# Causal attention on one core: one key tile for up to four query tiles a step, value products up to 512 columns wide

## The chip, the cores and the metric

The kernel runs on one core of a Trainium2 chip. The time is device microseconds of one execution; before the change three runs took 2228.47, 2224.61 and 2228.84, median 2228.47. The core's engines run side by side, each through its own queue in order: TensorE (PE; its weight loads are shown apart as PEld), VectorE (DVE), ScalarE (ACT), GpSimd (POOL), and SyncE (SP), whose queue issues nearly all DMAs. They wait for each other by semaphores.

## The reference, cut to what matters

Two layers over 1024 tokens of width 1024; layer 0 mixes by gating and convolution, layer 1 by attention with 16 heads of width 64, and each is followed by a convolutional feed-forward part. The change touches the attention alone:

```python
def dilated_attention(q, k, v):
    outs, lses = [], []
    for window, dilation in DILATED_PATTERNS:      # (128, 1), (512, 4), (2048, 16)
        o, lse = dilated_branch(q, k, v, window, dilation)
        outs.append(o)
        lses.append(lse)
    wts = jax.nn.softmax(jnp.stack(lses, axis=0), axis=0)
    return jnp.einsum('pbsh,pbshd->bshd', wts, jnp.stack(outs, axis=0))

# in the odd layer
qkv = (h @ odd_w_qkv[j]).reshape(bn, s, 3, ATTN_HEADS, HEAD_DIM)
q = rotary(qkv[:, :, 0], pos)
k = rotary(qkv[:, :, 1], pos)
v = qkv[:, :, 2]
o = dilated_attention(q, k, v).astype(x.dtype).reshape(bn, s, D_MODEL)
x = x + o @ odd_w_o[j]
```

Each branch is a softmax over the earlier keys at its distances, and the branches are mixed by their sums. That is one causal softmax in which a key counts as often as branches reach it; the kernel adds the logarithm of that count to the scores (the tile `mask`).

## The kernel before, in words

Nothing is scheduled by a compiler: the order on each engine is the order in which the Python code emits instructions. A `Ticker` counts ticks, and `after(n, fn)` emits `fn` n ticks later. A "unit" is a slice of independent matrix work (6 or 9 products of 512 columns) that is put between the parts of the attention as filler; `feed(x)` emits as many units as add up to x.

Float32 values are split for TensorE into a rounded high part (ACT, `hi_of`, line 196) and the rest (DVE, `lo_of`); products of two such values take three matmuls, and the value product below takes two, since v's parts stand side by side in the 128 weight columns.

The heads are taken in 8 pairs `hp`, and in each pair the heads e = 0 and 1. For each of these 16 passes:

- `scores` (lines 1431 and 1432) multiplies a query tile of 128 rows with all its earlier keys into PSUM banks `pss`; DVE adds the mask and takes the maximum (`top`), ACT takes the exponential (`ex`), and the tile `p` holds 128 queries by up to 1024 keys.
- `turn` transposes blocks of 128 x 128 of `p` through TensorE into a bank `ppt` (lines 1498, 1499). ACT and DVE split that bank into `tt`: the rounding one tick later, the rest two ticks later, which is ahead of the next step's transposes.
- `value` multiplies v with `tt` into a bank `po` (line 1518), two steps (`VLAG`) after the `turn`.

Before the change a step (hp, e, j, g) takes two query tiles (2j and 2j + 1) and two key tiles, so a value product has 256 columns and a step has four; 10 steps make a pass, in the order j = 3, 2, 0, 1. Where a block lies wholly above the diagonal it is zeroed by a POOL memset. The scores of a pair j are emitted four and three steps ahead of its first step. A step has two ticks, and each is fed with 0.6 units, 24 units a pair of heads.

The filler of a pair is the preparation of the next pair (`prepare`): 8 units each for k, q and v. After k's last unit `rotate` issues four DMAs on SP that bring the swapped halves into `sw`; six ticks later DVE multiplies `sw` with the sine, then the tile itself with the cosine (`rk` or `rq`), adds both, and ACT and DVE split the sum into `rh` and `rl`. For k, eight DMAs then make stacked copies; for q, four. k's rotation falls into the second head of a pair, q's into the first head of the next pair. During the seventh pair three `o` tiles are loaded back (`ot`), split on ACT and POOL (`o_split`), and in the last pair the filler is the first part of the output product (`psd`).

`stile` takes SBUF tiles from one pool of 23 (`p`, `tt`, the q and v of two pairs, raw weights, `sw` and more), and `bank` PSUM banks from a pool of 8. A new tile's first writer waits for the last reader of the tile that had the place before.

Of the kernel before, what the change touches and what calls it, by code (L numbers as in the profile page):

```python
# [58 lines left out]
LAST_RATE = 0.6  # L59
# [76 lines left out]
def block_kernel(ctx, tc, io, out):  # L136
# [1164 lines left out]
    def attention(x_dram, hT, then, late):  # L1301
# [113 lines left out]
        def scores(hp, e, qi, p):  # L1415
# [30 lines left out]
            def ex():  # L1446
# [6 lines left out]
        JORDER = (3, 2, 0, 1)  # L1453
        steps = [(hp, e, j, g) for hp in range(KT) for e in range(2) for j in JORDER
                 for g in range(j + 1)]
        first = {}
        for gi, (hp, e, j, g) in enumerate(steps):
            first.setdefault((hp, e, j), gi)
        LEAD = 4
        VLAG = 2  # L1460
# [6 lines left out]
        def do_scores(hp, e, j, odd):  # L1467
            n0, n1 = P * (2 * j + 1), P * (2 * j + 2)
            if not odd:
                if n0 + n1 <= S:  # L1470
                    t = stile(name="p")
                    ptiles[(hp, e, j)] = (t[:, :n0], t[:, n0:n0 + n1])
                else:
                    ptiles[(hp, e, j)] = (stile(name="p")[:, :n0], None)
            elif ptiles[(hp, e, j)][1] is None:
                ptiles[(hp, e, j)] = (ptiles[(hp, e, j)][0], stile(name="p")[:, :n1])
            scores(hp, e, 2 * j + odd, ptiles[(hp, e, j)][odd])
# [5 lines left out]
        def turn(hp, e, j, g):  # L1483

            pa, pb = ptiles[(hp, e, j)]
            last = 2 * j + 1
            pt = bank("ppt")
            tt = stile([P, 2, HALF], F32R, name="tt")
            tts[(hp, e, j, g)] = tt
            c = 0  # L1490
            for n, kb in enumerate(key_order(j, g)):
                ks = slice(kb * P, (kb + 1) * P)
                if kb == last:

                    c = P
                    pool.memset(f32v(tt[:, :, 0:P]), 0.0)
                else:
                    nc.tensor.transpose(pt[:, 256 * n:256 * n + P], pa[:, ks], ident)  # L1498
                nc.tensor.transpose(pt[:, 256 * n + P:256 * n + 256], pb[:, ks], ident)  # L1499
# [3 lines left out]
        def key_order(j, g):  # L1503
            return (2 * g + 1, 2 * g) if g == j else (2 * g, 2 * g + 1)

        def value(hp, e, j, g):
            v2 = sets[hp]["v"][e]
            half = j // 2
# [362 lines left out]
```

## Time and profile before

| what | before |
|---|---|
| runs, us | 2228.47, 2224.61, 2228.84 |
| the profiled execution | 2228.55 |
| its span | 2226.8 |
| granted clock of TensorE, mean | 0.995 |
| attention, first score product to last value product | 1036.8 to 1518.6 us of the span |
| value products (line 1518) | 640 of 256 columns |
| transposes for them (lines 1498, 1499) | 576 |
| splits of turned tiles, on ACT and on DVE | 160 and 160 |
| zeroing of blocks on POOL | 64, 312 ns each |

The profile is one execution. Its page gives busy times of the engines and the costliest groups; in a timeline each row has its start, its length, the engine, line and operation, the tiles written and read, and in brackets the idle time of the engine just before it with what ended it. A row for DVE names line 128, since a helper emits them all; they are told apart by tiles.

### The profile page before, as it was taken

What the parts mean: (1) busy time and instruction counts of PE and PEld (TensorE: products, weight loads), DVE (VectorE), ACT (ScalarE), POOL (GpSimd) and SP (SyncE); (2) the same over time, 40 slices, a digit from 0 to 9 for tenths busy, and PEclk for the clock granted to TensorE, in tenths of its full rate; (3) what the DMA queues carried; (4) which work ended last, traced back from release to release, by engine and by line L of the source; (5) the groups of instructions that cost most, each with busy time, mean ns of one, the idle gap of its engine ahead of it and who ended that gap; (6) DMA issues with size and microseconds to landing.
All of it is one profiled execution on the core that took longest, in us unless ns stands there. A gap on an engine that the chain in (4) does not pass through costs nothing.

```text
span 2226.8 us, 29232 instructions
## 1 busy us (share of the span) xinstructions
PE 2179.1 (98%) x10448; PEld 1822.1 (82%) x10448; DVE 1611.4 (72%) x2578; ACT 1096.7 (49%) x1667; POOL 700.8 (31%) x538
## 2 busy tenths in 40 slices
PE   7999899999999999999999999999999999999998
PEld 6888678888888888878888888788888888888886
DVE  6998668877777764665777777786787777778555
ACT  5345265544444445353555555554654444444532
POOL 0122023766665430040000000102466666653001
PEclk9999999999999999999999999999999999999999
DMA  5478411353534598446344444632134444349933
GB/s 191 113 134 184 161 67 67 133 183 128 181 142 158 175 352 321 142 168 152 94 106 116 124 106 122 187 126 97 67 133 156 171 144 178 132 158 347 363 131 116
DMA packets 138833, 352.13 MB, mean 158 GB/s; under 512 B 16448, under 2 KB 16832, under 8 KB 138688
## 3 DMA queue, kind: packets, MB, share of 16 engines
q1 hardware_dynamic: 133072, 329.90, 44.2%
q0 software_dynamic: 5616, 20.36, 4.6%
q8 instruction: 82, 1.34, 0.2%
q14 instruction: 63, 0.52, 0.1%
HBM read 216.01 MB, written 100.64 MB: 142 GB/s over the span
## 4 chain that ended last, share of the span: by engine, by line
PE 49%; DVE 2%; issue 2%; ACT 1%; POOL 0%; DMA 0%; SPq 0%; DVEq 0%; POOLq 0%; ACTq 0%
PE psd L1245 9%; PE psu L259 4%; PE psu L260 4%; PE psu L258 4%; PE po L1518 3%; PE psb L1069 3%; PE psb L1066 3%; PE psb L1067 3%; PE psc L1067 2%; PE psc L1069 2%; PE psc L1066 2%; PE pss L1432 2%; PE pss L1431 2%; PE ppt L1499 1%; PE ppt L1498 1%
## 5 line engine op out<-in xcount | busy, mean ns | idle before, releaser
L1245 PE MATMUL psd<-ab 128*128 128x512 f32 x1800 | 410.1, 389 | 0.0
L1245 PEld LDWEIGHTS psd<-ab 128*128 128x128 f32 x1800 | 337.5, 188 | 69.9
L258 PE MATMUL psu<-hTh,w 128*128 128x512 f32 (+1 forms) x592 | 236.9, 400 | 2.0 <-ACT hTh L196 2.0
L260 PE MATMUL psu<-hTh,w 128*128 128x512 f32 (+1 forms) x592 | 229.5, 388 | 0.0
L259 PE MATMUL psu<-hTl,w 128*128 128x512 f32 (+1 forms) x592 | 229.1, 387 | 0.2 <-DVE hTl L128 0.2
L196 ACT CAST ab<-ab 128x1024 fp32r<-128x1024 f32 x150 | 156.0, 1051 | 139.4 <-PE psd L1245 59.2
L128 DVE TENSOR_TENSOR ab<-ab,ab 128x1024 fp32r<-128x1024 f32 x150 | 192.1, 1334 | 33.4 <-ACT ab L196 33.0
L128 DVE TENSOR_TENSOR x<-psd,x 128x512 f32<-128x512 f32 x152 | 102.1, 686 | 136.7 <-PE psd L1245 110.1
L128 POOL MEMSET tt<- 128x256 f32 x64 | 19.9, 312 | 457.9 <-PE po L1518 260.8
L1103 ACT COPY sn<-psb 128x512 f32<-128x512 f32 x120 | 70.2, 586 | 170.2 <-PE psb L1069 127.4
L128 POOL TENSOR_TENSOR y<-y,y 128x512 f32<-128x512 f32 x66 | 95.6, 1448 | 182.5 <-DMA act<-y 116.4
L196 ACT CAST tt<-ppt 128x512 fp32r<-128x512 f32 (+1 forms) x160 | 86.6, 541 | 97.2 <-PE ppt L1499 87.6
L128 DVE TENSOR_TENSOR tt<-ppt,tt 128x512 fp32r<-128x512 f32 (+1 forms) x160 | 101.2, 633 | 45.8 <-ACT tt L196 44.6
L260 PEld LDWEIGHTS psu<-hTh,w 128*128 128x128 f32 x592 | 112.0, 189 | 23.1
L258 PEld LDWEIGHTS psu<-hTh,w 128*128 128x128 f32 x592 | 112.4, 190 | 19.0 <-ACT hTh L196 2.2
L259 PEld LDWEIGHTS psu<-hTl,w 128*128 128x128 f32 x592 | 112.6, 190 | 17.5 <-DVE hTl L128 0.5
L128 POOL TENSOR_TENSOR sm<-sm,mhalf 128x1 f32<-128x1 f32 (+2 forms) x38 | 31.2, 821 | 282.3 <-DVE sm L128 282.3
L128 POOL TENSOR_TENSOR s<-wr 128x512 f32<-128x512 f32 x40 | 83.0, 2076 | 116.8 <-DVE psa L128 100.8
L128 DVE TENSOR_TENSOR wl<-wr,wh 128x1024 fp32r<-128x1024 f32 x88 | 119.2, 1355 | 0.0
L1448 ACT ACTIVATE p<-p,sma 128x896 f32<-128x896 f32 (+7 forms) x128 | 99.5, 778 | 35.4 <-DVE sma L128 34.6
L128 DVE TENSOR_TENSOR pse<-psc,sn 128x512 f32<-128x512 f32 x40 | 27.9, 699 | 117.1 <-ACT sn L1103 117.1
L1518 PE MATMUL po<-tt,v 128*128 128x256 f32 x640 | 108.8, 292 | 3.8 <-DVE tt L128 2.9
(252 smaller groups left out, 5854.4 us busy)
## 6 DMA issues: line engine op xcount, KB each, us to landing
wr<-in_w_up_dram SPq DMA_DIRECT2D x88, 512.0 KB, 4.4
ab<-act SPq DMA_DIRECT2D x154, 256.0 KB, 5.4
act<-y SPq DMA_DIRECT2D x66, 512.0 KB, 2.9
wq<-in_w_down_dram SPq DMA_DIRECT2D x44, 512.0 KB, 5.3
wt<-wq SPq DMA_DIRECT2D x44, 512.0 KB, 4.6
ab<-wt SPq DMA_DIRECT2D x88, 256.0 KB, 5.4
ab<-in_w_down_dram SPq DMA_DIRECT2D x66, 256.0 KB, 5.6
wr<-in_w_qkv_dram SPq DMA_DIRECT2D x24, 512.0 KB, 3.8
```

Source lines behind the costliest of these rows:

```text
L128: return fn(*args, **kw)
L196: nc.scalar.copy(hi, src)
L258: nc.tensor.matmul(out_ap, st[0], mv[0], start=first, stop=False)
L259: nc.tensor.matmul(out_ap, st[0], mv[1], start=False, stop=False)
L260: nc.tensor.matmul(out_ap, st[1], mv[0], start=False, stop=last)
L1066: nc.tensor.matmul(ps, st[0], mv[0], start=f, stop=False, skip_group_check=True)
L1067: nc.tensor.matmul(ps, st[0], mv[1], start=False, stop=False, skip_group_check=True)
L1069: nc.tensor.matmul(ps, st[1], mv[0], start=False, stop=e, skip_group_check=True)
L1103: nc.scalar.copy(self.sn[key], self.b)
L1245: nc.tensor.matmul(ps, a[:, c], b[:, HALF:D], start=first and k == 0, stop=last and k == 2, skip_group_check=True)
L1448: nc.scalar.activation(p, p, AF.Exp, bias=sm[:, 2:3], scale=0.125, accum_out=lsum[hp][:, c:c + 1])
L1518: nc.tensor.matmul(po[:, c], v2[:, kb, :], tt[:, z, 256 * n:256 * n + 256], start=(g == 0 and n == 0 and z == 0), stop=(g == j and n == 1 ...
```

## The change

A step (hp, e, half, kb) now takes one key tile `kb` for all query tiles of a half (four tiles of 128, 512 queries) that can see it. The upper half has 8 steps and comes first, the lower half 4, so a pass has 12. A value product is 512 columns wide, and narrower towards the diagonal: 512 six times a pass, 384 twice, 256 four times, two products each. One block a half is zeroed, where 128 columns are left (the product then is 256 wide). `S_LEADS` says how many steps before a half's first step the scores of its four query tiles are emitted: 6, 5, 4, 3 for the upper half (tile 7 first), 5, 4, 3, 3 for the lower. The filler is fed by `shares`: a step with more work of its own (estimated in `work`) gets less; the sum over a pair stays 24 units, now over 24 steps or 48 ticks. In the last pair the shares are scaled by `LAST_RATE`. The steps of `finish_pair` are moved by two ticks.

```diff
-LAST_RATE = 0.6
+LAST_RATE = 0.5
+
+
+S_LEADS = ((5, 4, 3, 3), (6, 5, 4, 3))
+VLAG = 2
...
-        JORDER = (3, 2, 0, 1)
-        steps = [(hp, e, j, g) for hp in range(KT) for e in range(2) for j in JORDER
-                 for g in range(j + 1)]
+        steps = [(hp, e, half, kb) for hp in range(KT) for e in range(2)
+                 for half in (1, 0) for kb in range(4 * half + 4)]
...
-        for (hp, e, j), gi in first.items():
-            s_at.setdefault(gi - LEAD, []).append((hp, e, j, 0))
-            s_at.setdefault(gi - LEAD + 1, []).append((hp, e, j, 1))
+        for (hp, e, half), gi in first.items():
+            for n, lead in enumerate(S_LEADS[half]):
+                s_at.setdefault(gi - lead, []).append((hp, e, 4 * half + 3 - n))
...
-            c = 0
-            for n, kb in enumerate(key_order(j, g)):
-                ks = slice(kb * P, (kb + 1) * P)
-                if kb == last:
-
-                    c = P
-                    pool.memset(f32v(tt[:, :, 0:P]), 0.0)
-                else:
-                    nc.tensor.transpose(pt[:, 256 * n:256 * n + P], pa[:, ks], ident)
-                nc.tensor.transpose(pt[:, 256 * n + P:256 * n + 256], pb[:, ks], ident)
+            q0 = max(4 * half, kb)
+            c = (q0 - 4 * half) * P
+            if kb == 4 * half + 3:
+
+
+                pool.memset(f32v(tt[:, :, 2 * P:3 * P]), 0.0)
+            for qi in range(q0, 4 * half + 4):
+                at = (qi - 4 * half) * P
+                nc.tensor.transpose(pt[:, at:at + P],
+                                    ptiles[(hp, e, qi)][:, kb * P:(kb + 1) * P], ident)
             after(1, lambda: hi_of(tt[:, 0, c:], pt[:, c:]))
             after(2, lambda: lo_of(tt[:, 1, c:], pt[:, c:], tt[:, 0, c:]))
...
-            for n, kb in enumerate(key_order(j, g)):
-                for z in range(2):
-                    nc.tensor.matmul(po[:, c], v2[:, kb, :], tt[:, z, 256 * n:256 * n + 256],
-                                     start=(g == 0 and n == 0 and z == 0),
-                                     stop=(g == j and n == 1 and z == 1))
+            c = min(2, max(4 * half, kb) - 4 * half) * P
+            tt = tts.pop((hp, e, half, kb))
+            for z in range(2):
+                nc.tensor.matmul(po[:, c:], v2[:, kb, :], tt[:, z, c:],
+                                 start=kb == 0 and z == 0, stop=kb == last and z == 1,
+                                 skip_group_check=True)
...
             after(1, a)
-            after(2, b)
-            after(3, c)
-            after(4, d)
-            after(9, f)
+            after(4, b)
+            after(5, c)
+            after(6, d)
+            after(11, f)
...
-        per_tick = n_units / 40.0
+        n_steps = len(steps) // KT
+
+        def work(gi):
+            hp, e, half, kb = steps[gi % len(steps)]
+            n = 4 * half + 4 - max(4 * half, kb)
+            w = n * 0.09 + 2 * max(n, 2) * 0.057
+            return w + sum(0.114 * (a[2] + 1) for a in s_at.get(gi, ()))
+        base = KT // 2 * n_steps
+        works = [work(base + i) for i in range(n_steps)]
+        total = (sum(works) + n_units * 1.36) / n_steps
+        shares = [max(0.0, total - w) for w in works]
+        shares = [x * n_units / sum(shares) / 2 for x in shares]
```

On TensorE, around the end of the upper half in pass 8 (a transpose writes `ppt`, a value product `po`, a score product `pss`, filler `psu`), before the change:

```order
L258 MATMUL psu_10325<-hTh_7734,w_10009 128x512
L259 MATMUL psu_10325<-hTl_7735,w_10009 128x512
L260 MATMUL psu_10325<-hTh_7734,w_10009 128x512
L1518 MATMUL po_10186<-tt_10260,v_1430_9754 128x256 x4
L1431 MATMUL pss_10343<-k_9484,st_9728 128x512
L1432 MATMUL pss_10343<-k_9484,st_9728 128x512
L1431 MATMUL pss_10346<-k_9484,st_9728 128x512
L1432 MATMUL pss_10346<-k_9484,st_9728 128x512
L1499 MATMUL ppt_10355<-ident,p_10194 128x128
L1498 MATMUL ppt_10355<-ident,p_10194 128x128
L1499 MATMUL ppt_10355<-ident,p_10194 128x128
```

and now, where step 7's single transpose and step 8's four follow each other:

```order
L1497 MATMUL ppt_10294<-ident,p_9928 128x128
L1511 MATMUL po_10150<-tt_10232,v_1456_9724 128x384 x2
L1435 MATMUL pss_10306<-k_9425,st_9625 128x512
L1436 MATMUL pss_10306<-k_9425,st_9625 128x512
L1435 MATMUL pss_10309<-k_9425,st_9625 128x256
L1436 MATMUL pss_10309<-k_9425,st_9625 128x256
L1497 MATMUL ppt_10316<-ident,p_10204 128x128 x2
L1497 MATMUL ppt_10316<-ident,p_10155 128x128 x2
```

A step had four value products of 256 columns and filler about it; now the steps at the end of a half are short, and two sets of transposes stand close together.

On DVE, where the rotation of q stands in pass 8 (`sw` with the sine, `rq` with the cosine, `tt` the splits of turned tiles, the rows with `p` and `pss` the maxima), before the change:

```order
L128 TENSOR_TENSOR sw_10209<-sw_10209,sin_7723 128x1024
L128 TENSOR_TENSOR rq_10074<-rq_10074,cos_7722 128x1024
L128 TENSOR_TENSOR tt_10286<-ppt_10285,tt_10286 128x512
L128 ISA p_10306,sma_10307<-pss_10308,mask_7721 128x512
L128 ISA sma_10307 128x1
L128 ISA p_10306,sma_10307<-pss_10311,mask_7721,sma_10307 128x384
L128 ISA sma_10307 128x1
L128 TENSOR_SCALAR sma_10307<-sma_10307 128x1
L128 TENSOR_TENSOR o_9742<-o_9742,r_10251 128x1024
L128 TENSOR_TENSOR rq_10074<-rq_10074,sw_10209 128x1024
```

and now:

```order
L132 TENSOR_TENSOR sw_10109<-sw_10109,sin_7723 128x1024
L132 TENSOR_TENSOR rq_10037<-rq_10037,cos_7722 128x1024
L132 TENSOR_TENSOR tt_10164<-ppt_10163,tt_10164 128x512
L132 ISA p_10155,sma_10180<-pss_10181,mask_7721 128x384
L132 ISA sma_10180 128x1
L132 TENSOR_SCALAR sma_10180<-sma_10180 128x1
L132 TENSOR_TENSOR rq_10037<-rq_10037,sw_10109 128x1024
L132 TENSOR_TENSOR tt_10191<-ppt_10190,tt_10191 128x512
```

The same rotation now stands in the first half of the pass, behind the split of step 2 and ahead of those of steps 3 and 4; before it stood behind the maxima of the next half's scores, in the sixth of ten steps. The four DMAs that fill `sw` stand on SP behind the eight copies of k in both.

At the end of pass 15, TensorE before the change:

```order
L1518 MATMUL po_13097<-tt_13182,v_1963_12402 128x256 x4
L1498 MATMUL ppt_13225<-ident,p_13140 128x128
L1499 MATMUL ppt_13225<-ident,p_13140 128x128
L1498 MATMUL ppt_13225<-ident,p_13140 128x128
L1499 MATMUL ppt_13225<-ident,p_13140 128x128
L1518 MATMUL po_13097<-tt_13202,v_1963_12402 128x256 x4
L1499 MATMUL ppt_13242<-ident,p_13140 128x128
L1498 MATMUL ppt_13242<-ident,p_13140 128x128
L1499 MATMUL ppt_13242<-ident,p_13140 128x128
L1518 MATMUL po_13248<-tt_13214,v_1963_12402 128x256 x4
L1518 MATMUL po_13248<-tt_13226,v_1963_12402 128x256 x4
L1518 MATMUL po_13248<-tt_13243,v_1963_12402 128x256 x4
```

and now:

```order
L1497 MATMUL ppt_13053<-ident,p_12770 128x128
L1511 MATMUL po_12963<-tt_13032,v_2021_12292 128x384 x2
L1497 MATMUL ppt_13061<-ident,p_13013 128x128 x2
L1497 MATMUL ppt_13061<-ident,p_12968 128x128 x2
L1511 MATMUL po_12963<-tt_13043,v_2021_12292 128x256 x2
L1497 MATMUL ppt_13071<-ident,p_13013 128x128
L1497 MATMUL ppt_13071<-ident,p_12968 128x128 x2
L1511 MATMUL po_12963<-tt_13054,v_2021_12292 128x256 x2
L1497 MATMUL ppt_13082<-ident,p_12968 128x128 x2
L1511 MATMUL po_13086<-tt_13062,v_2021_12292 128x512 x2
L1497 MATMUL ppt_13091<-ident,p_12968 128x128
L1511 MATMUL po_13086<-tt_13072,v_2021_12292 128x384 x2
```

In both no filler stands among the last steps; four such steps before, seven now, with fewer columns each. On POOL the zeroing of step 7's tile (`tt_13054`) stands behind the last split of an `o` tile.

More of the change, by code (lines that the diff above doesn't have):

```diff
@@ L1451, in scores, with do_scores @@
             after(2, ex, 2)
-        JORDER = (3, 2, 0, 1)
-        steps = [(hp, e, j, g) for hp in range(KT) for e in range(2) for j in JORDER
-                 for g in range(j + 1)]
+        steps = [(hp, e, half, kb) for hp in range(KT) for e in range(2)
+                 for half in (1, 0) for kb in range(4 * half + 4)]
         first = {}
[L1457 to L1460, printed above, removed]
+        for gi, (hp, e, half, kb) in enumerate(steps):
+            first.setdefault((hp, e, half), gi)
         s_at = {}
-        for (hp, e, j), gi in first.items():
-            s_at.setdefault(gi - LEAD, []).append((hp, e, j, 0))
-            s_at.setdefault(gi - LEAD + 1, []).append((hp, e, j, 1))
+        for (hp, e, half), gi in first.items():
+            for n, lead in enumerate(S_LEADS[half]):
+                s_at.setdefault(gi - lead, []).append((hp, e, 4 * half + 3 - n))
         ptiles = {}
[L1467 to L1472, printed above, removed]
-                else:
[L1474 to L1477, printed above, removed]
+        def do_scores(hp, e, qi):
+            n = P * (qi + 1)
+            if qi >= 4:
+                ptiles[(hp, e, qi)] = stile(name="p")[:, :n]
+            elif qi % 2:
+                t = stile(name="p")
+                ptiles[(hp, e, qi)] = t[:, :n]
+                ptiles[(hp, e, qi - 1)] = t[:, n:2 * n - P]
+            scores(hp, e, qi, ptiles[(hp, e, qi)])
         tts = {}
@@ L1500, in turn, with value @@
             after(1, lambda: hi_of(tt[:, 0, c:], pt[:, c:]))
             after(2, lambda: lo_of(tt[:, 1, c:], pt[:, c:], tt[:, 0, c:]))
-        def key_order(j, g):
-            return (2 * g + 1, 2 * g) if g == j else (2 * g, 2 * g + 1)
-        def value(hp, e, j, g):
+        def value(hp, e, half, kb):
             v2 = sets[hp]["v"][e]
-            half = j // 2
-            new = j in (3, 0) and g == 0
-            if new:
+            last = 4 * half + 3
+            if kb == 0:
                 pos[0] = bank("po")
@@ L1522, in value @@
+            tt = tts.pop((hp, e, half, kb))
[3 more added lines that the diff above has]
+                                 skip_group_check=True)
+            if kb == last:
                 if hp not in outs_o:
@@ L1527, in ev @@
                     vec.tensor_tensor(o, po[HD:P, :], o, op=ALU.add)
-                    if e == 1 and j == 1:
+                    if e == 1 and half == 0:
                         finish_pair(hp)
@@ L1624, in attention @@
         tk.until(lambda: "v" in sets[0])
-        for gi in range(-LEAD, 0):
+        for gi in range(-max(S_LEADS[1]), 0):
             for a in s_at.get(gi, ()):
@@ L1647, in attention @@
         for step in steps[-VLAG:]:
-            feed(2 * per_tick)
+            feed(2 * LAST_RATE)
             tick(2)
```

20 lines of the change are left out of this document (7 added, 13 removed).

## The prediction

> **What bounds the kernel now.** I read the page first, then the busy time of the engines by stretches of the attention stage.
>
> ```profile
> span 2226.8 us, 29232 instructions
> PE 2179.1 (98%) x10448; PEld 1822.1 (82%) x10448; DVE 1611.4 (72%) x2578; ACT 1096.7 (49%) x1667; POOL 700.8 (31%) x538
> ...
> PEclk9999999999999999999999999999999999999999
> ```
>
> The execution took 2228.55 us by the clock of the runs, 1.75 more than its span and 0.08 over the median of 2228.47. All my sums start from 2228.55. TensorE is busy 98% at full clock, so the order of the other engines counts only where it leaves TensorE waiting.
>
> ```profile
> 1340.00:1400.00 60.00, 60.00 (x353) 52.19 (x352) 45.48 (x104) 34.89 (x72) 2.18 (x7) 1.00 0.44 110
> 1400.00:1460.00 60.00, 54.47 (x307) 47.12 (x306) 46.94 (x98) 34.69 (x67) 10.26 (x10) 0.94 0.76 227
> 1460.00:1520.00 60.00, 58.95 (x363) 51.57 (x362) 44.24 (x113) 35.67 (x73) 12.45 (x14) 1.00 0.20 63
> ```
>
> After the stretch and its length come PE, PEld, DVE, ACT and POOL, then clock and DMA. In the normal stretch PE never idles, DVE has 14.5 us of 60 free and ACT 25. Idle time exists in pass 12 (the seventh pair's first head; I number the 16 passes from 0) and at the end of pass 15. So a normal pass can gain only through fewer streamed columns, and any new wait is a loss.
>
> **Term 1, the matmuls.** A busy row overlaps the next one, so I take start to start.
>
> ```profile
> 1423.96 0.65 PE L1518 MATMUL po<-tt,v 128*128 128x256 f32 x4
> 1424.44 0.40 PE L1431 MATMUL pss<-k,st 128*128 128x512 f32 x1
> 1424.68 0.40 PE L1432 MATMUL pss<-k,st 128*128 128x512 f32 x1
> 1424.91 0.34 PE L1431 MATMUL pss<-k,st 128*128 128x384 f32 x1
> 1425.09 0.34 PE L1432 MATMUL pss<-k,st 128*128 128x384 f32 x1
> 1425.27 0.27 PE L1499 MATMUL ppt<-ident,p 128*128 128x128 f32 x1
> 1425.37 0.27 PE L1498 MATMUL ppt<-ident,p 128*128 128x128 f32 x1
> ```
>
> A product of 256 columns takes 0.48/4 = 0.12 us, one of 512 0.235, one of 384 0.18, a transpose 0.11. Before: 640 x 0.12 = 76.8. After, per pass 12 of 512, 4 of 384 and 8 of 256, so 192 x 0.235 + 64 x 0.18 + 128 x 0.12 = 72.0. Transposes, score products and filler keep their counts. **Term 1: -4.8** (-4 to -6 by the rounding of these starts).
>
> The splits of the turned tiles get 192 instead of 160 instructions a side over the same columns.
>
> ```profile
> L196 ACT CAST tt<-ppt 128x512 fp32r<-128x512 f32 x96 | 55.9, 582 | 72.1 <-PE ppt L1499 63.0 <-PE pss L1432 8.8
> L128 DVE TENSOR_TENSOR tt<-ppt,tt 128x512 fp32r<-128x512 f32 x96 | 65.9, 687 | 33.8 <-ACT tt L196 33.5
> L128 DVE TENSOR_TENSOR tt<-ppt,tt 128x384 fp32r<-128x384 f32 x64 | 35.4, 553 | 12.0 <-ACT tt L196 11.1
> L128 DVE CUSTOM_DVE_ANT_0 p<-pss,mask 128x512 f32<-128x512 f32 x63 | 43.0, 682 | 9.6 <-PE pss L1432 9.6
> L128 DVE TENSOR_SCALAR sma<-sma 128x1 f32<-128x1 f32 x127 | 19.5, 154 | 4.4
> ```
>
> 687 at 512 and 553 at 384 leave 0.15 us per instruction: 4.8 us more DVE in all, 0.3 a pass, beside 14.5 free in 60; ACT alike. POOL loses 32 memsets. I cost these at nothing; if DVE were never free they would cost their 4.8.
>
> **Term 2, the stall of pass 12.**
>
> ```profile
> 1427.20 1.22 DVE L128 TENSOR_TENSOR sw<-sw,sin 128x1024 f32<-128x1024 f32 x1 [4.13 <-DMA sw<-rq]
> ...
> 1431.35 0.33 PE L1499 MATMUL ppt<-ident,p 128*128 128x128 f32 x1 [2.80 <-DVE tt L128]
> ...
> 1432.57 0.63 PE L260 MATMUL psu<-hTh,w 128*128 128x512 f32 x1
> 1432.99 0.63 PE L258 MATMUL psu<-hTh,w 128*128 128x512 f32 x1
> ...
> 1442.16 1.01 PE L1518 MATMUL po<-tt,v 128*128 128x256 f32 x3 [2.73 <-DVE tt L128]
> ...
> 1444.89 0.63 PE L258 MATMUL psd<-w,o 128*128 128x512 f32 x1
> 1445.32 0.43 PE L259 MATMUL psd<-w,o 128*128 128x512 f32 x1
> ```
>
> DVE stood 4.13 us for the half-swapped copy of q (sw), its queue ran late, and PE stalled 2.80 and 2.73 us. Behind each, 512-column products started 0.42 apart instead of 0.235; over some 3.4 us each that is 1.6 lost. Together 8.7. The Trainium skill (TensorE: Matmul & The Clock Gate, section What's actually happening) lets the clock fall after an idle window of about 3.4 us; this trace shows it after 2.80. By the page no wait expected below costs clock; by the trace one near 2.8 would add 1.6, which the upper end holds.
>
> In pass 12 an o tile's load stood ahead of the swap on SP; now the swap's four DMAs come first, as in a normal pass. So pass 12 becomes a normal even pass with two more 1.22 us weight splits in DVE's way.
>
> **Term 3, the even passes.** Passes with e = 0 prepare the next pair's q, and the change moves that against DVE's order.
>
> ```profile
> 1046.18 0.27 PE L1498 MATMUL ppt<-ident,p 128*128 128x128 f32 x1
> ...
> 1047.38 0.50 SPq L1366 DMA_DIRECT2D k<-rh  x1
> ...
> 1061.10 1.23 DVE L128 TENSOR_TENSOR sw<-sw,sin 128x1024 f32<-128x1024 f32 x1 [3.83 <-DMA sw<-rq]
> ...
> 1346.95 0.50 SPq L1366 DMA_DIRECT2D k<-rh  x1
> ...
> 1355.22 3.61 SPq L1336 DMA_DIRECT2D sw<-rq  x4
> ...
> sw<-rq SPq DMA_DIRECT2D x4, 128.0 KB, 3.7
> ...
> 1363.11 1.23 DVE L128 TENSOR_TENSOR sw<-sw,sin 128x1024 f32<-128x1024 f32 x1 [0.38 <-issue]
> 1364.25 1.22 DVE L128 TENSOR_TENSOR rq<-rq,cos 128x1024 f32<-128x1024 f32 x1
> 1365.39 0.68 DVE L128 TENSOR_TENSOR tt<-ppt,tt 128x512 fp32r<-128x512 f32 x1
> 1365.99 0.68 DVE L128 CUSTOM_DVE_ANT_0 p<-pss,mask 128x512 f32<-128x512 f32 x1
> ```
>
> The swap stands on SP behind eight k copies. From the first copy to the landed swap it is 13.7 us in the first pass (1047.38 to 1061.10). In the later one it is 16.2 at most; its last swap goes out near 1358.2 and a swap lands a median 3.7 later, which gives 15.0. I take **14.2** from between, ends 13.7 and 16.2.
>
> When does the first copy go out now? In an odd pass DVE works without a gap from the maximum of tile 7, whose scores end 14.0 us before the next pass (rows counted as in term 1), to the rotated k: the order has maximum (1.7), split (0.3), maximum (1.5), product (1.14), split (0.15), maximum (1.45), two products (2.3), 8.5 in all, then ACT's rounding, 1.1. So it goes out at -4.4 and the swap lands at **M = +9.8**, in the new pass's time. In passes 2, 6 and 10 a copy's buffer is first freed at -3.5: M = 10.7. DVE reaches the product with sw near +8: 12 transposes, 18 filler, 6 value and 2 score products (6.9), then one maximum. So it waits some 2 us, and queued behind are the splits that TensorE needs.
>
> From M, DVE by the order and these rows: 1.14 + 1.14 + 0.6 (split 3) + 0.7 + 1.15 + 0.6 (split 4) + 0.54 + 0.41 + 1.14 + 0.47 (split 5) + 1.7 + 0.4 (split 6) = 10.0. The transposes of step 8 write the PSUM bank that split 6 reads, and PE comes to them at 19.6: 26 transposes (2.8), 16 value products (3.2), 20 score products (3.8), 42 filler (9.8). So PE waits M + 10.05 - 19.6: 0.25 in passes 4 and 8, 1.15 in 2, 6 and 10. Before, the shortest way from the point in PE's order where such a split can start to the next writing of its bank was 1.8 us, counted alike; now it is 1.2 (two value products, four scores, one transpose). The value products of steps 3 to 5 wait only from M = 10.4 on. In pass 0 the scores lead by 3.4 us more, so its copies go out at about -2.2 (before, 1047.38 against a pass start at 1046.18, 1.2 behind); M = 12.0, step 8 comes at 19.0, wait 3.0. Pass 12: M = 9.8, two splits more: 22.1 - 19.6 = 2.5. Sum: 0.5 + 3.45 + 3.0 = **+7.0**, and pass 12 2.5 instead of 8.7, **-6.2**. With M 0.5 earlier: 4.5 and 2.0; with M 2.0 later: 19 and 4.5.
>
> Odd passes: split 8 is done 0.7 us and split 9 0.9 us before its value product, by the same count. I cost them at nothing; below zero nothing is to be had, as PE idles nowhere there.
>
> The pool of 23 SBUF tiles has up to six score tiles in it instead of five, so ACT's rounding of a turned tile now often waits for a value product of an older step. That product stands ahead in PE's order, and the tile's own comes 5.4 us or more behind its transposes, against 0.6 + 0.7 of work: nothing, and if DVE is late by M at the same time, it is within the ends of M. The steps that close a pair keep their places counted in steps; nobody on PE waits for them but one transpose four ticks on.
>
> **Term 4, the tail.**
>
> ```profile
> 1515.17 2.38 POOL L128 TENSOR_TENSOR o<-ot,o 128x1024 fp32r<-128x1024 f32 x1 [0.45 <-ACT o L196]
> ...
> 1517.48 0.32 POOL L128 MEMSET tt<- 128x256 f32 x1
> ...
> 1516.36 0.61 PE L1518 MATMUL po<-tt,v 128*128 128x256 f32 x3 [0.17 <-DVE tt L128]
> 1517.86 0.74 PE L1518 MATMUL po<-tt,v 128*128 128x256 f32 x4 [0.88 <-POOL tt L128]
> ```
>
> The last steps have no filler between them, and PE lost 1.05: the zeroing of a turned tile stood behind a 2.38 us split on POOL. Now seven steps stand bare, 4.8 us of PE rows from step 5's transposes on. Split 5 ends 0.7 after PE wants it (an addition and two maxima stand ahead). ACT first takes two exponentials and a 1.05 us rounding of o, so split 6 is 1.3 late. POOL's o split starts behind that rounding, the memset of step 7 behind it: 1.5 late. Two short waits at the end: 0.6. That is 4.1 against 1.05: **+3.0** (0 if the o split slips ahead, 4 if not).
>
> **Sum:** -4.8 - 6.2 + 7.0 + 3.0 = -1.0, so **2227.5 us**.
>
> **Rivals.**
> *The swap is in time (faster).* If k's copies go out 1.5 us sooner, or DVE comes late to the product by itself, no even pass waits, 12 included: -4.8 - 8.7 + 3.0 = -10.5, 2218; with the tail unchanged 2215. For it: before, DVE waited only 0.38 in the later passes. Against: there the product came 15.8 us behind the first copy, now 8 + 4.4 = 12.4.
> *The swap is later (slower).* At M = 11.8, the end that 1346.95 to 1363.11 allows, waits at the value products of steps 3 and 4 and at step 8's bank add to 19 in passes 0 to 10 and 4.5 in 12: -4.8 + 19 - 4.2 + 3.0 = +13, 2241.5. It decides once M passes 10.5. For it: hops between engines, which I left out; against: the first pass's 13.7.
> *A matmul costs the same at any width.* Then 256 products fewer save 256 x 0.12 = 30.7 instead of 4.8: 2201.5. The rows above, 0.12 against 0.235, speak against it. Nearest to it stands the Trainium skill (same page, section Back-to-back issue gap), with about 81 ns at 128 and 131 at 512 columns in a stream; the trace disagrees.
>
> **How the numbers follow.** A run tells about 0.2%, 4.5 us, from no change. Forecast 0.43, own range 2222 to 2233 (0.37 within 0.2%, 0.04 faster, 0.02 slower); swap in time 0.29; swap later 0.26; one cost at any width 0.02. Faster 0.35, same 0.37, slower 0.28. The range takes both ends of M: 2215 to 2241.
>
> **What would show it.** Term 1: value products in three widths with the starts above. Term 3: DVE waiting 1.5 to 2.5 us for sw<-rq in each even pass, and PE's transposes waiting for DVE tt once a pass at step 8. Term 2: no o load between k's copies and the swap, PE's waits in pass 12 below 3 us. Term 4: PE waiting for POOL's memset at the end. It is wrong if even passes show no wait (2218), or value products wait in the middle of them (2241).

## The result, and the profile after

The changed kernel takes 2233.64 us (median of 8 runs) against 2229.12 for the kernel before (8 runs beside it): ratio 1.0024, 95% interval 1.0014 to 1.0034, so it is slower by about 5 us. The profiled execution of the changed kernel took 2236.17 us, the highest of its eight and 2.5 above their median; 7.6 more than the 2228.55 of the execution profiled before. The two traces are compared as they are; some 3 us of their difference lie within the spread of single executions.

The first lines of the changed kernel's page:

```profile
span 2234.4 us, 28705 instructions
PE 2180.6 (98%) x10192; PEld 1809.6 (81%) x10192; DVE 1611.1 (72%) x2610; ACT 1098.1 (49%) x1699; POOL 691.4 (31%) x506
```

Busy times hardly moved, so the answer lies in TensorE's idle time. What TensorE waited for in the attention (each row: waiter and its tile, what ended the wait, us in total, times, longest), first in the kernel before:

```profile
PE po L1518 <- DVE tt L128: 2.9, 2, 2.7
PE ppt L1499 <- DVE tt L128: 2.8, 1, 2.8
PE po L1518 <- POOL tt L128: 0.9, 1, 0.9
```

and in the changed kernel:

```profile
PE psu L262 <- DVE tt L132: 8.6, 7, 5.0
PE po L1511 <- POOL tt L132: 1.6, 2, 1.3
PE pss L1435 <- DVE tt L132: 1.0, 1, 1.0
PE po L1511 <- DVE tt L132: 0.8, 3, 0.4
PE pss L1435 <- DVE sma L132: 0.6, 1, 0.6
PE po L1511 <- ACT tt L200: 0.5, 1, 0.5
PE psd L264 <- POOL o L132: 0.5, 1, 0.5
```

Idle time doubled from 6.6 to 13.6 us, and 8.6 of it is one new kind: a product of the filler that waits for DVE's split of a turned tile, once in each even pass.

To place the difference I cut the trace at the first transpose of each pass and take from each pass the time that its matmuls' columns need at the usual start-to-start times (0.109, 0.119, 0.176 and 0.233 us at 128, 256, 384 and 512 columns, medians of the trace). What is left is called "over the columns": waits, and slower products behind them. A pass without waits comes to -0.1. The granted clock of the changed kernel's attention was 0.50 from 1063.4 to 1070.2 (pass 0) and from 1520.8 to the end (pass 15), and 1.00 elsewhere.

| part, us | before | after | change | forecast |
|---|---|---|---|---|
| columns of the whole attention | 472.6 | 467.7 | -4.9 | -4.8 |
| pass 0, over its columns | -0.2 | 6.9 | +7.1 | +3.0 |
| passes 2, 4, 6, 8, 10 | -0.6 | 4.5 | +5.1 | +4.0 |
| odd passes 1 to 11 | -0.6 | 0.0 | +0.6 | 0 |
| pass 12 | 8.9 | 5.4 | -3.5 | -6.2 |
| passes 13 to 15 | 1.5 | 4.6 | +3.1 | +3.0 |
| outside the attention | | | +0.2 | 0 |
| sum | | | +7.6 | -1.0 |

**The columns.** Pass 7 has no wait in either kernel. Its first transpose and that of pass 8, before:

```profile
1256.91 0.27 PE L1498 MATMUL ppt<-ident,p 128*128 128x128 f32 x1
...
1286.59 0.27 PE L1498 MATMUL ppt<-ident,p 128*128 128x128 f32 x1
```

and after:

```profile
1268.06 0.60 PE L1497 MATMUL ppt<-ident,p 128*128 128x128 f32 x4
...
1297.41 0.60 PE L1497 MATMUL ppt<-ident,p 128*128 128x128 f32 x4
```

29.68 became 29.35, 0.33 less with the same filler and scores. Worked out from the medians above, little of it comes from the width itself: two products of 256 columns take 0.238, one of 512 takes 0.233, which is 0.06 for the twelve of a pass. Most of it, 0.24, is 512 columns fewer in a pass, because two zeroed blocks are left of four.

**Pass 0**, rows of the changed kernel's timeline (start, length, engine, line, operation, tiles, and in brackets the idle time before):

```profile
1045.32 0.55 DVE L132 CUSTOM_DVE_ANT_0 p<-pss,mask 128x384 f32<-128x384 f32 x1
...
1046.62 1.22 DVE L132 TENSOR_TENSOR rk<-rk,sw 128x1024 f32<-128x1024 f32 x1
...
1047.91 1.05 ACT L200 CAST rh<-rk 128x1024 fp32r<-128x1024 f32 x1 [0.25 <-ACT p L1452]
...
1048.97 0.60 PE L1497 MATMUL ppt<-ident,p 128*128 128x128 f32 x4
...
1048.99 0.50 SPq L1370 DMA_DIRECT2D k<-rh  x1
...
1057.56 3.73 SPq L1340 DMA_DIRECT2D sw<-rq  x4
...
1063.26 1.23 DVE L132 TENSOR_TENSOR sw<-sw,sin 128x1024 f32<-128x1024 f32 x1 [6.79 <-DMA sw<-rq]
...
1066.27 0.79 PE L262 MATMUL psu<-hTh,w 128*128 128x512 f32 x1 [4.98 <-DVE tt L132]
1066.86 0.63 PE L263 MATMUL psu<-hTl,w 128*128 128x512 f32 x1
```

The pass starts at 1048.97 and k's first copy goes out at +0.02, not at -2.2 as forecast. In the kernel before, the maxima of two score tiles stood ahead of k's sum on DVE, now those of all four of the upper half do; the last of them are those of the row at 1045.32 and of the 256 columns that follow it. The sum ends at 1047.84 instead of 1046.21. (An exponential stands ahead of k's rounding on ACT too, but it ends before the sum does.) From the first copy to DVE's start on the landed swap it is 14.27 us (14.2 forecast), so DVE starts the product with sw at +14.3 (12.0 forecast), works off two products and a split, and TensorE stands for 4.98 us. Behind that wait products are 0.4 apart or more, at a granted clock of 0.50, and 1.8 us go there.

**A later even pass** (6, it starts at 1236.96):

```profile
1241.28 0.59 ACT L200 CAST tt<-ppt 128x512 fp32r<-128x512 f32 x1 [1.71 <-PE po L1511]
...
1241.90 0.69 DVE L132 TENSOR_TENSOR tt<-ppt,tt 128x512 fp32r<-128x512 f32 x1 [2.99 <-ACT tt L200]
...
1247.19 1.22 DVE L132 TENSOR_TENSOR sw<-sw,sin 128x1024 f32<-128x1024 f32 x1
1248.34 1.22 DVE L132 TENSOR_TENSOR rq<-rq,cos 128x1024 f32<-128x1024 f32 x1
1249.47 0.68 DVE L132 TENSOR_TENSOR tt<-ppt,tt 128x512 fp32r<-128x512 f32 x1
...
1250.21 0.50 PE L262 MATMUL psu<-hTh,w 128*128 128x512 f32 x1 [0.38 <-DVE tt L132]
```

ACT's rounding of step 1's tile waits for a value product, though its transposes are done: its place in the pool of 23 is not free. DVE stands 2.99 us for that, and reaches the product with sw at +10.2 instead of +8; the swap lands just then, and DVE waits 0.14 for it. From +7 to +27 DVE has no idle time above 0.25 us in this pass. The filler's first product of step 5 writes the bank that split 3 reads, and split 3 stands behind the two products.

**Pass 12** (starts at 1419.6, granted clock 1.00 throughout), TensorE's rows that wait:

```profile
1433.26 0.50 PE L262 MATMUL psu<-hTh,w 128*128 128x512 f32 x1 [0.75 <-DVE tt L132]
...
1436.78 0.50 PE L1435 MATMUL pss<-k,st 128*128 128x512 f32 x1 [0.96 <-DVE tt L132]
...
1441.46 0.50 PE L1435 MATMUL pss<-k,st 128*128 128x512 f32 x1 [0.61 <-DVE sma L132]
...
1447.90 0.50 PE L1511 MATMUL po<-tt,v 128*128 128x256 f32 x2 [0.38 <-POOL tt L132]
...
1452.60 0.50 PE L264 MATMUL psd<-w,o 128*128 128x512 f32 x1 [0.46 <-POOL o L132]
```

and **the tail**:

```profile
1517.77 0.44 PE L1511 MATMUL po<-tt,v 128*128 128x384 f32 x1 [0.41 <-DVE tt L132]
...
1519.13 0.85 PE L1511 MATMUL po<-tt,v 128*128 128x256 f32 x2 [0.48 <-ACT tt L200]
...
1521.56 0.80 PE L1511 MATMUL po<-tt,v 128*128 128x256 f32 x2 [1.25 <-POOL tt L132]
```

The tail waits where the forecast had it: split 5 by DVE, split 6 by ACT, the memset behind the o split on POOL. The waits are shorter than forecast (2.1 us in the three rows for 3.5), and slower products behind them make up for it.

### The profile page after: what moved, and what is told of

Same layout as the page of the kernel before. It is cut to its first block, busy times and chain, and to the rows that moved or that the text cites. A ratio compares the mean times of both kernels' runs of the same rounds, so it can differ in the third digit from the quotient of the medians.

```text
span 2234.4 us, 28705 instructions
## 1 busy us (share of the span) xinstructions
PE 2180.6 (98%) x10192; PEld 1809.6 (81%) x10192; DVE 1611.1 (72%) x2610; ACT 1098.1 (49%) x1699; POOL 691.4 (31%) x506
## 4 chain that ended last, share of the span: by engine, by line
PE 43%; DVE 5%; issue 2%; SPq 2%; ACT 1%; DMA 1%; POOL 1%; DVEq 0%; POOLq 0%; ACTq 0%
PE psd L1249 9%; PE psu L262 3%; PE psu L264 3%; PE psb L1073 3%; PE psu L263 3%; PE psb L1070 3%; PE psb L1071 3%; PE po L1511 2%; PE ppt L1497 2%; PE psc L1073 2%; PE psc L1070 2%; PE psc L1071 2%; PE pss L1435 1%; PE pss L1436 1%; PE psa L1073 1%
## 5 line engine op out<-in xcount | busy, mean ns | idle before, releaser
L262 PE MATMUL psu<-hTh,w 128*128 128x512 f32 (+1 forms) x592 | 240.8, 407 | 10.6 <-DVE tt L132 8.6
L132 POOL MEMSET tt<- 128x256 f32 x32 | 9.9, 313 | 453.6 <-PE ppt L1497 185.3
L132 DVE TENSOR_TENSOR tt<-ppt,tt 128x512 fp32r<-128x512 f32 x192 | 105.1, 552 | 48.3 <-ACT tt L200 47.2
L1452 ACT ACTIVATE p<-p,sma 128x1024 f32<-128x1024 f32 (+7 forms) x128 | 99.4, 779 | 71.5 <-DVE sma L132 69.2
L200 ACT CAST tt<-ppt 128x512 fp32r<-128x512 f32 x192 | 90.5, 476 | 85.6 <-PE ppt L1497 54.5
L1511 PE MATMUL po<-tt,v 128*128 128x512 f32 (+2 forms) x384 | 109.1, 366 | 3.0 <-POOL tt L132 1.6
```

The lines of the kernel that those rows point to most:

```text
L132: return fn(*args, **kw)
L200: nc.scalar.copy(hi, src)
L262: nc.tensor.matmul(out_ap, st[0], mv[0], start=first, stop=False)
L1452: nc.scalar.activation(p, p, AF.Exp, bias=sm[:, 2:3], scale=0.125, accum_out=lsum[hp][:, c:c + 1])
L1511: nc.tensor.matmul(po[:, c:], v2[:, kb, :], tt[:, z, c:], start=kb == 0 and z == 0, stop=kb == last and z == 1, skip_group_check=True)
```

## The experiments

Two theories stood at the start. **Late swap**: the even passes wait because q's swap lands late. **DVE is full**: in an even pass DVE has more to do between +7 and +27 than fits, so that what stands ahead of the splits counts, whenever the swap lands. **Slots** is a part of the second: the tight pool makes DVE late to begin with. Ratios are to the kernel before, run beside each kernel, with 95% intervals.

### 1. q's swap on POOL's queue

```diff
-                    nc.sync.dma_start(sw[32 * b:32 * b + 32, :],
+                    (q or nc.sync).dma_start(sw[32 * b:32 * b + 32, :],
...
-            fins = [lambda: rotate(rk, fin_k, soon), lambda: rotate(rq, fin_q, soon)]
+            fins = [lambda: rotate(rk, fin_k, soon),
+                    lambda: rotate(rq, fin_q, soon, None if soon else nc.gpsimd)]
```

> The four DMAs of q's swap go out on POOL's queue as soon as q is complete (about +2.6 us in a pass) instead of behind the copies of k on SP; nothing else is moved. Theory 'late swap': the waits that come from its landing go, so TensorE's 5.15 us in pass 0 and what passes 8 and 10 have above passes 2 to 6 (0.45 and 0.8) fall to about 0.45 each; with the half-clock products behind the long one some 7 to 8 us are saved, about 2226. Theory 'DVE's order' (two products of 1.14 us stand ahead of split 3 whatever the swap does): 0.43 to 0.54 stay in each even pass. Rival 'a queue of POOL is no faster': swap lands as late, 2233 to 2234.

Ratio 1.0051 (1.0039 to 1.0064), slower than the changed kernel. Pass 8 of this run, which starts at 1296.82:

```profile
1299.96 1.94 POOL L1340 DMA_DIRECT2D sw<-rq  x4 [4.50 <-PE ppt L1497]
...
1309.02 1.23 DVE L132 TENSOR_TENSOR sw<-sw,sin 128x1024 f32<-128x1024 f32 x1 [2.08 <-DMA sw<-rq]
...
1312.03 0.50 PE L262 MATMUL psu<-hTh,w 128*128 128x512 f32 x1 [2.34 <-DVE tt L132]
```

The swap goes out at +3.1, and DVE can still start on it only at +12.2, later than behind k's copies on SP (+10.6); those copies were under way. In pass 0 DVE starts earlier (+11.7 instead of +14.3). So both expectations of an early swap failed, but the run gives the wait at other starting points. TensorE's loss at step 5 against DVE's start on the product with sw, both kernels, us after the pass's start:

| | pass 2 | 4 | 6 | 8 | 10 | 0 |
|---|---|---|---|---|---|---|
| changed kernel, start | 10.13 | 10.17 | 10.23 | 10.62 | 10.97 | 14.28 |
| loss | 0.46 | 0.48 | 0.54 | 0.92 | 1.27 | 5.15 |
| swap on POOL, start | 10.85 | 11.03 | 11.33 | 12.20 | 11.02 | 11.71 |
| loss | 1.18 | 1.34 | 1.64 | 2.50 | 1.33 | 2.57 |

In passes 2 to 10 the loss is the start less 9.7, ten times within 0.03; in pass 0 the start less 9.1. In passes 2 and 4 of the changed kernel DVE did not wait for the swap at all. So late swap explains pass 0 and a share of 8 and 10; the 0.45 us of the others is DVE's own lateness.

### 2. q's products three ticks later

```diff
-            after(6 - 2 * soon, m2)
-            after(7 - 5 * soon, m1)
-            after(8 - 3 * soon, add)
+            after(6 - 2 * soon + late, m2)
+            after(7 - 5 * soon + late, m1)
+            after(8 - 3 * soon + late, add)
...
```

The rounding, the rest and the stacking follow with the same `late`, which is 3 for q from the second pair on.

> The three products of q's rotation and what follows them are put three ticks later, so that splits 3 and 4 stand ahead of them on DVE; the swap's DMAs stay. Both 'late swap' and 'DVE's order' expect the step-5 waits of all even passes to go (6.9 us in pass 0, 4.5 in passes 2 to 10, about 1 in pass 12): about 2221. If DVE is short of time in these passes as a whole, the waits only move to splits 5 and 6 and the time stays above 2228.

Ratio 1.0019 (1.0011 to 1.0028). Pass 0 falls from 6.9 over its columns to 3.6; passes 2 to 10 stay (4.5 and 4.7), and the wait has moved. Pass 6, the transposes of step 8:

```profile
1253.62 0.63 PE L1497 MATMUL ppt<-ident,p 128*128 128x128 f32 x4 [0.65 <-DVE tt L132]
```

A wait that changes its place when the order changes, and not its size, is what a full engine gives.

### 3. The kernel before, o loads behind the swap

```diff
-                if n >= 16 and n - 16 < len(O_GROUPS[0]):
-                    ots[n - 16] = o_load(n - 16)
+                if n >= 17 and n - 17 < len(O_GROUPS[0]):
+                    ots[n - 17] = o_load(n - 17)
```

> The kernel before, with the o tiles' loads one unit later, so that in pass 12 the swap's DMAs stand ahead of the first of them on SP. Theory 'the o load in front of the swap made the stall of pass 12': its 8.9 us above the sum of its columns go, about 2220. Rival 'contention or DVE's weight splits made it': DVE still waits some 4 us and the time stays within 3 us of before's 2229.

Ratio 0.9994 (0.9985 to 1.0003); pass 12 falls only from 8.9 to 7.2. DVE does not wait for sw any more and the first stall of 2.80 is gone, but the second has grown:

```profile
1436.21 8.10 POOL L128 TENSOR_TENSOR o<-ot,o 128x1024 fp32r<-128x1024 f32 x3 [8.83 <-ACT o L196]
...
1436.37 3.38 DVE L128 TENSOR_TENSOR w<-wr,w 128x1024 fp32r<-128x1024 f32 x1
...
1440.27 1.01 PE L1518 MATMUL po<-tt,v 128*128 128x256 f32 x3 [3.27 <-DVE tt L128]
```

The load ahead of the swap made one of the two stalls. In the other, a weight split took 3.38 us on DVE instead of 1.22 beside POOL's o splits (3.40 in the kernel before); run 12 follows that up.

### 4. A shorter lead of the scores

```diff
-S_LEADS = ((5, 4, 3, 3), (6, 5, 4, 3))
+S_LEADS = ((5, 4, 3, 3), (5, 4, 3, 3))
```

> The changed kernel with the lead of the upper half's scores cut from 6, 5, 4, 3 steps to 5, 4, 3, 3, so that fewer score tiles hold slots of the pool of 23. Theory 'slots' (ACT's rounding waits for value products to free a tile, which makes DVE reach the product with sw at +10.1 instead of +8): ACT's waits for value products fall from 21.6 us to under 10, and the 0.45 us of passes 2 to 6 go, some 2 us. If slots do not matter, the waits of the even passes stay as they are; the time then changes only by what DVE's later maxima cost.

Ratio 1.0130 (1.0116 to 1.0143). ACT's waits for value products fell as expected:

```profile
ACT tt L200 <- PE po L1511: 6.8, 3, 3.0
```

against 21.6 in the changed kernel, but the later maxima cost far more: 18.5 over the columns in passes 2 to 10, and 7.0 in the odd ones. The run says nothing of slots; it shows that the long lead carries the new order.

### 5. One tile less

```diff
-S_TILES = 23
+S_TILES = 22
```

> The changed kernel with 22 instead of 23 tiles in the pool that score tiles, turned tiles and the rotation's tiles share. Theory 'slots' (a turned tile waits for a value product to free its place, which keeps DVE idle for 3 us early in an even pass and makes it reach the product with sw at +10.1): with one place less DVE starts that product later, by 1 us or more, and TensorE's waits in the even passes grow by as much, 6 to 10 us in all, 2238 to 2242. If places do not matter: within 2 us of the changed kernel.

Ratio 1.0088 (1.0074 to 1.0102). Of that, 4.6 us lie ahead of the attention (its first score product at 1041.0 instead of 1036.4; the other runs of the new order with 23 tiles have it at 1033.0 to 1037.3). In the attention it costs 6 us: even passes 6.4 instead of 4.5, odd 2.6 instead of 0.0, pass 12 7.2 instead of 5.4. ACT's waits for value products in the changed kernel:

```profile
ACT tt L200 <- PE po L1511: 21.6, 14, 2.2
```

and in this one:

```profile
ACT tt L200 <- PE po L1511: 52.6, 36, 3.5
```

So places matter. But passes 4 and 8 stayed as they were, so how much of DVE's lateness the 23 places make stays open; no run has a pool with more.

### 6 to 8. q's products on POOL; the tail's last o split later; both

```diff
-                vec.tensor_tensor(st["sw"], st["sw"], sin, op=ALU.mult)
+                (eng or vec).tensor_tensor(st["sw"], st["sw"], sin, op=ALU.mult)
...
-            after(12, lambda: o_split(hp, ot))
+            after(12 + 8 * (hp == KT - 2), lambda: o_split(hp, ot))
```

The first pair of lines is that of run 6 (the other two products alike, `eng` is `pool` for q), the second that of run 7.

> The three products of q's rotation go to POOL, which is idle in these passes; the rounding of q and what follows is put 5 ticks later (8 for the second pair), since POOL is slower. Theory 'DVE is full': in an even pass DVE has no idle time from +7 us to +27, so 3.4 us less work on it takes away every wait that the products move about; the waits of passes 2 to 10 go (4.5 us), pass 0's 6.9 go but for 0.5, pass 12's by 1 to 2: about 12 us under the changed kernel, a ratio to before near 0.997. Rival 'POOL and DVE share a path': products on POOL slow DVE's own work (a DVE subtraction took 3.40 instead of 1.22 us beside POOL's splits in pass 12 of before), the waits stay, and the ratio stays at 1.002 or above. Rival 'slots': sw and rq hold their tiles 5 ticks longer and ACT waits more for them.

Ratio 1.0006 (0.9998 to 1.0015). In passes 0 to 11 every kind of wait that the products moved about is gone: pass 0 is 0.0 over its columns instead of 6.9, passes 2 to 10 together 0.0 instead of 4.5 (waits of 0.2 are left in passes 6 and 10, at other places). Pass 6 of this run (it starts at 1227.1) on POOL:

```profile
1237.44 2.41 POOL L132 TENSOR_TENSOR sw<-sw,sin 128x1024 f32<-128x1024 f32 x1 [11.70 <-PE ppt L1497]
1239.80 2.41 POOL L132 TENSOR_TENSOR rq<-rq,cos 128x1024 f32<-128x1024 f32 x1
...
1242.29 2.40 POOL L132 TENSOR_TENSOR rq<-rq,sw 128x1024 f32<-128x1024 f32 x1
```

The products are twice as slow there, and nobody waits for them. For passes 2 to 10 this settles "DVE is full" together with run 2, in which DVE mostly found the swap landed and the loss stayed. In pass 0 the edit takes both the products and the wait for the swap off DVE, so it does not tell the two theories apart there; the table of run 1 does. The ratio of 0.997 that was expected was missed by pass 12, which got worse, 12.0 instead of 5.4: there ACT's rounding starts only when POOL's product with the cosine ends (1421.92), and DVE and TensorE stand behind it.

```profile
1421.95 0.59 ACT L200 CAST tt<-ppt 128x512 fp32r<-128x512 f32 x1 [5.14 <-POOL rq L132]
```

> The changed kernel with the last loaded o tile's split put 8 ticks later, behind the steps that stand bare at the end; nothing else is moved. Theory 'the memset of step 7 and split 6 stand behind that o tile on POOL and ACT': of the tail's 4.9 us above its columns (1.75 before) the 1.4 for POOL and 0.65 for ACT go, with the half-clock products behind them 2 to 3 us less. If the bare steps are bound by their own chain of transposes, rounding, split and product, the waits only change their names and less than 1 us goes.

Ratio 1.0037 (1.0024 to 1.0049). Passes 13 to 15 are 4.1 over their columns instead of 4.6, and the waits have other places: the o tile's rounding on ACT and its split on POOL now stand ahead of the steps at the very end. Under 1 us, as the second expectation had it; the time as a whole was no better.

> Both edits of the two runs before: the sum of their gains if they are independent, as the places (passes 0 to 12, end of pass 15) say: by 'DVE is full' a ratio to before near 0.996, by 'POOL and DVE share a path' near 1.001.

Ratio 1.0013 (1.0004 to 1.0022), so the second edit adds nothing to the first.

### 9 and 10. q's products on POOL where POOL is free

```diff
-            fins = [lambda: rotate(rk, fin_k, soon), lambda: rotate(rq, fin_q, soon)]
+            fins = [lambda: rotate(rk, fin_k, soon),
+                    lambda: rotate(rq, fin_q, soon, pool if 0 < hp < KT - 1 else None,
+                                   8 if hp == 1 else 5 if 1 < hp < KT - 1 else 0)]
...
-                pool.memset(f32v(tt[:, :, 2 * P:3 * P]), 0.0)
+                (vec if hp == KT - 1 else pool).memset(f32v(tt[:, :, 2 * P:3 * P]), 0.0)
```

> As the run with q's products on POOL, but pair 7 (pass 12) keeps them on DVE, where POOL has the o splits to do, and the last pair's memsets go to DVE instead of standing behind o splits on POOL. Theory 'DVE is full in the even passes': passes 0 to 10 stay free of waits (as measured: -11 us), pass 12 is back at 5.4 us above its columns instead of 12.0, the tail loses POOL's 1.4 and some half-clock products: 8 us under that run, a ratio to before of 0.997, so faster than both kernels. Rival 'pass 12 is bad whatever stands ahead': its excess stays above 10 and the ratio above 1.000.

2220.53 us beside 2226.43: ratio 0.9971 (0.9959 to 0.9982), below the kernel before and, by the two ratios, below the changed kernel (1.0024). Passes 0 to 11 are free (0.1, -0.1 and 0.0 over the columns), pass 12 is at 5.3, the tail's 4.6 at 3.0. The filler's group in this run waits for DVE 0.7 us instead of 8.6:

```profile
L262 PE MATMUL psu<-hTh,w 128*128 128x512 f32 (+1 forms) x592 | 240.0, 405 | 2.7 <-ACT hTh L200 2.0 <-DVE tt L132 0.7
```

> The run before it, with the low part of two weight splits of pass 12 on POOL instead of DVE (2 x 1.22 us off DVE). Theory 'DVE is short in pass 12 as in the other even passes': its 5.4 us fall to 3 or less. Rival 'POOL and DVE share a path' or 'memset and o splits on POOL come late by it': pass 12 stays or grows.

Ratio 0.9980 (0.9971 to 0.9989); pass 12 rises from 5.3 to 5.9. Two splits less on DVE did not help: DVE's product with sw started beside POOL's weight split and took 2.97 us.

### 11. The same order, value products at most 256 wide

```diff
-                nc.tensor.matmul(po[:, c:], v2[:, kb, :], tt[:, z, c:],
-                                 start=kb == 0 and z == 0, stop=kb == last and z == 1,
-                                 skip_group_check=True)
+                for a, b in ((c, 256), (256, 512)) if c < 256 else ((c, 512),):
+                    nc.tensor.matmul(po[:, a:b], v2[:, kb, :], tt[:, z, a:b],
+                                     start=kb == 0 and z == 0, stop=kb == last and z == 1,
+                                     skip_group_check=True)
```

The two column halves open their sums apart, and the sums of this kernel are no longer those of the attention; why was not traced. Number, size and order of its products are as stated, and only its time is read.

> The changed kernel in its own order, but every value product wider than 256 columns is issued as two, split at column 256. Term 1 (wide products gain 4.8 us over all passes through their columns): the odd passes without waits grow by 0.24 to 0.34 us, all of it by 4 to 5 us where TensorE is not waiting, a little less where waits take it up: ratio to before near 1.004. Rival 'a matmul costs the same at any width': 12 x 2 + 4 x 2 = 32 more products a pass at 0.12 would be 2.4 to 3.8 us a pass, 40 to 60 in all.

Ratio 1.0048 (1.0035 to 1.0062). The odd passes without waits take 29.64 us instead of 29.35, and the attention 3.2 us more, the rest being taken up by shorter waits. So adding up start-to-start times, which is how Term 1 was made, holds (0.29 for the 0.24 to 0.34 expected), and the rival of one cost at any width falls: 16 more products a pass would have cost 1.9 us. (The 32 of the expectation counts each twice.) Most of the 0.29 is not the difference between 512 and 256 columns: by the medians the twelve products of 512 give 0.06, and the four of 384, cut into 128 and 256, give 0.21, since a product of 128 columns takes 0.109, nearly as long as one of 256.

### 12. The kernel before, without POOL's three o splits

```diff
-            split(o, oh, ol, pool if hp < KT - 1 else None)
+            split(o, oh, ol, pool if len(O_GROUPS[0]) <= hp < KT - 1 else None)
```

> The kernel before with the o loads behind the swap, and the low parts of the first three o tiles on DVE instead of POOL. Theory 'a DVE operation with all operands in SBUF that meets one of POOL waits for its end' (3.38 instead of 1.22 us in pass 12): that weight split is back at 1.22 us, and of pass 12's 7.2 us above its columns about 2.2, with the half-clock products behind the stall 3 to 4, go, less what the three splits of 1.22 us add to DVE. Rival 'DVE is simply too full in pass 12': its stall stays near 3.5 us or grows, and the time with it.

Ratio 0.9996 (0.9987 to 1.0005); pass 12 stays at 7.2 over its columns. The weight split is quick again, and the stall stays:

```profile
1435.27 1.22 DVE L128 TENSOR_TENSOR w<-wr,w 128x1024 fp32r<-128x1024 f32 x1
...
1438.14 1.01 PE L1518 MATMUL po<-tt,v 128*128 128x256 f32 x3 [4.31 <-DVE tt L128]
```

The rival forecast this, and the theory's gain did not come. But the run puts about as much on DVE as it takes off: two of the three o splits now stand ahead of the turned tile's split, 1.1 us each. What would be left with neither on DVE was not run; the 2.2 us that the weight split was longer in run 3, taken from its wait of 3.27, would leave 1.1, which is an estimate. So the second stall comes from what DVE has to do in pass 12; how much of it is the sharing with POOL stays open.

### 13. The kernel before with run 9's two edits

> The kernel before with the two edits of the fastest run so far: q's products of pairs 1 to 6 on POOL, and the last pair's memsets on DVE. Theory 'DVE is full in the even passes only in the new order': before, TensorE waits nowhere in passes 0 to 11, so nothing is gained there (under 0.3 us); the tail's memset wait of 0.9 us goes, pass 12 stays near 8.9 above its columns: ratio 0.999 to 1.000. Rival 'the edits help any order': passes 0 to 11 get shorter here too, and the ratio comes near 0.997, so that the changed order had no part in the gain.

Ratio 0.9995 (0.9986 to 1.0004). Passes 0 to 11 are as before to 0.2 us. Pass 12 is at 6.6 over its columns where 8.9 was expected, and the tail is as before: its wait for POOL's memset is gone, and others have taken its place. So DVE's lack of time in passes 0 to 10 belongs to the new order; relieved of it, the new order is 0.24% ahead of the old one with the same edits (0.9971 against 0.9995).

## Why the prediction was wrong, by its own steps

It forecast 2227.5, a change of -1.0; the traces show +7.6 and the medians +4.5, inside the range but on the other side of no change. The direction was lost in two places, **pass 0 of Term 3** (4.1 us too low) and **what Term 2 leaves in pass 12** (2.9 over forecast, 5.4 for 2.5).

- **Term 1** was right: -4.9 for -4.8, 0.33 in a pass without waits; run 11 confirms the way it was added up.
- **Term 3, pass 0, is the step that failed most.** "Its copies go out at about -2.2" took it that the scores' longer lead leaves k's rotation where it was. It does not: the maxima of two more score tiles stand ahead of it on DVE. The copies went at +0.02, the swap landed at +14.3, not 12.0, and the wait was 5.15 for 3.0. To that come 1.8 us at half clock, which the forecast had only for the upper end. The chain behind (14.2 us from copy to swap, then DVE's queue) was right.
- **Term 3, passes 2 to 10**, was nearly right in size by luck (3.7 lost at step 5 for 3.95; the rest of its 5.1 are small waits and slower products elsewhere, at a granted clock of 1.00) and half wrong in its cause. The swap landed as forecast (+9.7 to +10.9 for +9.8 and +10.7), but DVE came to it at +10.1, not +8, and waited 0.02 to 0.87 us for it, not 1.5 to 2.5. Two steps failed. "DVE has 14.5 us of 60 free" is an average: from +7 to +27 of an even pass it has nothing free. And the pool of 23 tiles, costed at nothing, holds ACT's rounding back; run 5 shows that it counts. The wait then fell on the filler's product at step 5, a next writer of split 3's bank which the forecast had not looked at, not on step 8's transposes, which wait in run 2. That also removes the rival "swap in time": passes 2 to 6 would have lost their 0.45 us with any swap.
- **Odd passes**, costed at nothing, lost 0.6: in passes 1 and 3 a value product stands six filler products earlier than in 5 to 11, and split 9 comes 0.44 late.
- **Term 2** took both stalls of pass 12 for one cause. Run 3 shows that the o load ahead of the swap made the first; the second came from DVE's work in this pass, its sharing with POOL included, and was not the swap's. TensorE's waits for DVE in the changed pass 12 came to 2.3 us (2.5 forecast), but by luck: they are three, at filler and score products, and not one at step 8's transposes. Not forecast were POOL's two (0.38 and 0.46) and the shorter waits and slow first products behind all five, the rest of the 5.4. No product ran at half clock there: the granted clock was 1.00.
- **Term 4** had the three waits at the places named, but its +3.1 for +3.0 is partly luck. Idle time in pass 15 grew by only 1.2 us, from 1.05 to 2.2, where 3.0 was forecast; the waits were 0.41, 0.48 and 1.25 for 0.7, 1.3 and 1.5. The other 1.9 are slower products, most of them behind 1520.8 at a granted clock of 0.50, which the forecast did not have. Run 9 took POOL's part away.

## What to carry to other kernels

Look for an engine's free time in the stretch where the new order needs it, not in an average over a window: 24% free was none at all for 20 us of every other pass. When scores or loads are given a longer lead, everything that is queued behind the work now moved ahead comes later, transfers included. And a wait that moves when the order changes, and does not shrink, asks for work to be taken off the engine: three products on an idle engine at half the speed won 11 us in passes 0 to 11, where moving them in time won 3.

## What the runs showed of the hardware that was not expected

A DVE operation with both inputs in SBUF that starts beside a two-input operation of POOL's ends some 1.1 us after POOL's does: 3.38 us instead of 1.22 in run 3, 2.97 in run 10, and 1.22 again in run 12. One that had begun before POOL's kept its 1.22 (in the kernel before, at 1437.12), and so did those beside POOL's memsets; DVE's splits and maxima, which read PSUM, took the same time beside POOL as alone (0.69 at 512 columns). The Trainium skill (SBUF — State Buffer, section Who interferes with whom) says that a DVE instruction with two SBUF inputs contends with a GpSimd one that reads SBUF; the trace agrees.

A wait of 2.34 us cost clock in pass 8 of run 1: products went at 0.23 for 1.3 us more, then 0.43 apart for some 3 us. A wait of 2.41 in pass 0 of the same run cost none. So waits well under 3 us can already cost clock, and whether they do depends on more than their length. In these traces the stretches at a granted clock of 0.50 last 3.41 us or twice that, and within a trace they all begin on one grid of 3.41 us. The 2.34 us lay almost wholly in one cell of it (2.1 us between 1309.89 and 1313.30, half clock from there to 1316.71); the 2.41 us were divided over two, 1.9 and 0.5. How much idle time a cell can hold is not shown: 1.4 us was followed by half clock in run 2 (pass 12), 1.6 was not in run 7 (pass 0).

DMAs issued earlier from another queue landed later (run 1, pass 8: out from +3.1 on, used from +12.2 on, against +5.5 and +10.6 on SP). k's copies were under way in both; what slowed the four was not traced further.
